# One transpose per pair for q and k in two units, and another order at the end of a hybrid attention block

## The chip, the cores and the metric

The kernel runs on one core of a Trainium2 chip. The metric is the device time of one execution in microseconds; lower is better. The time before is the median of three runs.

## The reference

The block has two attention branches over one RMS-normed input, `x` being 2048 positions of 1024 features in float32:

```
h    = rms_norm(x, norm_gain);  proj = h @ w_in
qa, ka, va, qb, kb, vb, ga, gb, mg = split(proj)
ya   = banded_attention(qa, ka, va, 128, ..., sink)       # A: 8 q heads, 2 kv heads
ya   = ya * silu(ga)
for g, (window, dilation) in ((128, 1), (512, 4), (2048, 16)):
    o, l = dilated_group(qb[g], kb[g], vb[g], window, dilation)   # B: 8 heads each
yb   = sum(softmax(lses) * outs) * silu(gb)
gates = sigmoid(mg + b_merge)
x    = x + (gates[0] * (ya @ w_branch_a) + gates[1] * (yb @ w_branch_b)) @ w_out
```

q and k of each head are RMS-normed over 64 features, and a bias by relative position is added to the scores.

## The kernel before

Every float32 operand is split into two float16 parts, and a product is made of three float16 products. The program is written out in full in one order: the code puts each step into a heap with a planned time (`at`), and `until` emits what is due. The planned times decide only the order of instructions on each engine; on the chip, engines wait for each other through semaphores.

**The attention stage.** It runs through 14 units (`UNITS`): two of kind A (4 q heads, 1 k and 1 v head, positions in 16 subsets of 128) and twelve of kind B (2 heads, one of the three dilations). A unit has 8 pairs, a pair has two subsets of 128 positions. `Pair.matmuls` projects them (line 697), and `Pair.plan` sets the steps behind it: `evac_qk`, the norm (`square` to `gain`), the split into `spl` (`hi`, `lo`), and `swap`, in which GpSimd (POOL) copies the k columns once more with the two parts exchanged (line 779). `spl` then holds two subsets of 6 blocks of 128 columns. `Pair.turn` (line 787) transposes it with one DMA per subset, issued on SyncE's queue (SP), into a tile `kq` of 6 blocks; there are 6 such buffers (`KQ_BUFS`), and for the first subset of a class of kind B with more than one subset a separate ring `kq0` of 3.

For each subset there are items of two heads. An item of kind A in the middle of the sequence reads its own `kq` and those of both neighbours (`Item.logits`, line 847), makes probabilities on VectorE and ScalarE, splits them (lines 875, 879), transposes them with a DMA on SP (line 885) into `pt16`, shown as `pt`, and multiplies them with v (`Item.values`, line 896). An item of kind A that has two neighbours transposes 1536 columns; a `kq` transpose has 768. SP issues all these transposes and all loads and stores of the stage, in the order of the program. Scores of an item come before the values of earlier items, so the transposes of several items are under way.

**The last stage.** Branch projections (`Branch`) and the output projection (`Out`) are made in 16 groups of 7 products each. A group makes four output blocks out of seven products (Strassen's scheme in Winograd's form). The products accumulate in three PSUM banks: products 0, 3, 5 and 6 in bank 0, products 1 and 4 in bank 2, product 2 in bank 1. `after` follows each product: in a `Branch`, 0, 1 and 3 are copied by ScalarE and 2, 4, 5 are added to a copy by VectorE (line 1854), 6 is used directly; in an `Out`, each product is added to the output tile by VectorE (`put`, line 2000), and four of the puts are followed by a store (line 2003). A product that accumulates into a bank waits until the value before it has been read.

`run` orders them: 0, 1, then the delayed product 5 of the group before (`late`), 2, 3, the delayed 6, 4; products 5 and 6 go into `pending`. `flush` emits what is pending, before the output group of step 6 and at the very end. So the products of the two groups in question come as (5', 6' being those of the neighbour): 0 1 5' 2 3 6' 4, later 5 6. `m_build` makes the operands `mf` of the output products out of the results of the branch groups.

Of the kernel before, what the change touches and what calls it, by code (L numbers as in the profile page):

```python
# [22 lines left out]
F16 = mybir.dt.float16  # L23
I32 = mybir.dt.int32
AF = mybir.ActivationFunctionType
OP = mybir.AluOpType
# [6 lines left out]
NT = S // 128  # L33
# [65 lines left out]
X_US = dict(look=0.25, land=4.3, next=1.45, late=.12, sq=1.14, st=.17, ln=.2, nw=.75, sc=1.24, tr=.8, hi=.5, lo=.62, gs=2.1, pw=1.3,  # L99
            gh=1.06, gl=1.26, mm=.217, th=.6, gt=.63, us=.83, uh=.75, ul=.82, ag=1.0, tl=1.3)  # L100
XT_BUFS = 14
KQ_BUFS = 6
VT_BUFS = 10
PT_BUFS = 4
N_BIAS_A = 384
# [3 lines left out]
def block_kernel(tc, x, w_units, w_gate, w_mrg, w_out, w_bra, w_brk, gain, qkg, sink, bias_a, bias_b, b_merge, out):  # L109
    nc = tc.nc  # L110
    V = nc.vector
    A = nc.scalar
    G = nc.gpsimd
    T = nc.tensor
# [12 lines left out]
    def ucol():  # L127

        ucount[0] += 1
        return ubuf[:, ucount[0] - 1:ucount[0]]  # L130
# [252 lines left out]
    def at(t, f, *args):  # L383
        seq[0] += 1
        heapq.heappush(heap, (t, seq[0], f, args))

    now = [0.0]

    def until(t):
        while heap and heap[0][0] <= t:  # L390
            now[0], _, f, args = heapq.heappop(heap)
            f(*args)
# [121 lines left out]
    class Order:  # L514
# [17 lines left out]
        def run(self):  # L532
            while self.steps:
                best = {}
                for n, s in self.steps.items():
                    t = self.start(n)
                    if t is not None:
                        best.setdefault(s[0], []).append((t, s[3], n))
                eng, c = min(best.items(), key=lambda e: min(e[1])[0])
                t0 = min(c)[0]  # L540
                t, _, n = min((x for x in c if x[0] <= t0 + (0 if eng == "T" else X_US["look"])), key=lambda x: x[1])
                eng, us, _, _, f, args, _ = self.steps.pop(n)
                self.end[n] = self.free[eng] = t + us
                at(t, f, *args)
# [15 lines left out]
    for t in range(NT):  # L560
        g = groups[t]
# [8 lines left out]
        for h in range(2):  # L570
            k = 2 * t + h
# [52 lines left out]
    wk = main.enter_context(tc.tile_pool(name="wk", bufs=2, reuse_waits="tile"))  # L624
# [55 lines left out]
    class Pair:  # L680
# [7 lines left out]
        def matmuls(self, i):  # L688
            un, (r, c) = self.un, self.subsets[i]
            self.ps[i] = ps = pj_p.tile([128, 512], F32, name="pj")  # L690
            out = []
            for a, b, aligned in ((0, 128, True), (128, 384, False)) if un.shift else ((0, 384, True),):
                h, lo = subset(0, un.g, r, c, aligned), subset(1, un.g, r, c, aligned)
                k = 0
                for ch in range(NCH):
                    for lhs, rhs in ((h, un.wh), (h, un.wl), (lo, un.wh)):
                        out.append(lambda lhs=lhs, rhs=rhs, ch=ch, a=a, b=b, k=k: T.matmul(  # L697
                            ps[:, a:b], lhsT=lhs[:, ch, :], rhs=rhs[:, ch, a:b], start=(k == 0), stop=(k == 23)))
                        k += 1
            return out  # L700
# [78 lines left out]
                G.tensor_copy(sp[:, i, nh:, :, :], sp[:, i, nq:nh, ::-1, :])  # L779

        def turn(self):
            for i, s in enumerate(self.subsets):
                if self.un.shift and s[1] == 0:
                    kq = wk.tile([128, 6, 128], F16, name="kq0", bufs=3)
                else:
                    kq = wk.tile([128, 6, 128], F16, name="kq", bufs=KQ_BUFS)
                nc.sync.dma_start_transpose(out=kq[:], in_=self.sp[:, i].rearrange("p a b c -> p (a b c)"))
                self.un.kq[s] = kq


    class Item:
# [415 lines left out]
    for u in range(NU + 1):  # L1207
        t = 8 * u
# [8 lines left out]
    for k in range(8):  # L1217
        u = 3 + k
        t = 8 * u
# [10 lines left out]
    t = 0  # L1230
    while t < NPAIR or heap or any(k >= t for k in fill):
        u, j = divmod(t, 8)
# [24 lines left out]
        for share, f, i, args in streams:  # L1257
            until(pos)
            if args is None:
                mm, after = f(i), ()  # L1260
            else:
                mm, after = f(*args)
            for k, m in enumerate(mm):
                until(pos + share * k / len(mm))
                m()
            pos += share
            for k, a in enumerate(after):
                at(pos + GATE[k], a)
# [35 lines left out]
    def bank():  # L1304
        return ps_p.tile([128, 512], F32, name="fps")

    (sb, ib), (so, io) = (scales[k] for k in "bo")
    ysg, yig, msc, bnd, i_o = (ucol() for _ in range(5))
# [420 lines left out]
    for k in range(2):  # L1729
        g = LAST - 2 + k  # L1730
# [36 lines left out]
    def y_build(s, k, b, b0=None):  # L1767
        load, sums, hi, lo = y_parts(s, k)
        at(b if b0 is None else b0, load)
        for n in range(4):  # L1770
            at(b + Y_S + .4 * n, sums, n)
        for n in range(7):
            at(b + Y_S + .9 + .7 * n, hi, n)
            at(b + Y_S + 1.7 + .7 * n, lo, n)
# [40 lines left out]
    class Seven:  # L1815
# [8 lines left out]
        def after(self, i):  # L1824
            b, r = self.b, self.r
            if i == 0:
                self.copy(0, b[0])
            elif i == 1:
                self.copy(2, b[2])
            elif i == 2:  # L1830
                self.sum(0, b[1])
            elif i == 3:
                self.copy(1, b[0])
            elif i == 4:
                self.sum(1, b[2])
            elif i == 5:
                self.sum(2, b[0])
            else:
                self.last(b[0])
# [16 lines left out]
    def emit(g, i):  # L1856
        until(pos[0])
        mm = g.mm(i)
        us = g.mm_us
        for k, m in enumerate(mm):  # L1860
            until(pos[0] + us * k / len(mm))
            m()
        pos[0] += us
        until(pos[0])
        now[0] = pos[0]
        g.after(i)

    pending = []

    def late():  # L1870
        if pending:
            emit(*pending.pop(0))

    def run(g):
        emit(g, 0)
        if g.n == 1:
            late()
            return
        emit(g, 1)
        late()  # L1880
        emit(g, 2)
        emit(g, 3)
        late()
        emit(g, 4)
        pending.extend(((g, 5), (g, 6)))

    def flush():
        while pending:
            pos[0] += .3
            late()  # L1890
# [5 lines left out]
    WO = rp.tile([128, 7, 2, 4, 512], F16, name="WO")  # L1896
# [78 lines left out]
    class Out(Seven):  # L1975
# [11 lines left out]
        def matmuls(self, i, ps, fresh):  # L1987
            m = mf[self.s, i]
            out = []
            for p in range(4):  # L1990
                for ml, wl in ((0, 0), (0, 1), (1, 0)):
                    k = len(out)
                    out.append(lambda p=p, ml=ml, wl=wl, k=k: T.matmul(  # L1993
                        ps[:], lhsT=m[:, ml, p, :], rhs=WO[:, i, wl, p, :],
                        start=(fresh and k == 0), stop=(k == 11), skip_group_check=True))
            return out

        def put(self, h, n, b, store=False):
            t = self.x[h, n]
            at(now[0] + .2, lambda: V.scalar_tensor_tensor(t[:], b[:], i_o[:], t[:], OP.mult, OP.add))  # L2000
            if store:
                t0 = 128 * self.s + 1024 * h
                at(now[0] + 1.0, lambda: nc.sync.dma_start(
                    out=out[t0:t0 + 128, 512 * n:512 * n + 512], in_=t[:]))

        def after(self, i):
            b = self.b
            for h, n, k, store in (((0, 0, 0, False),), ((1, 1, 2, False),), ((0, 0, 1, True),), ((0, 1, 0, False),),
                                   ((0, 1, 2, True),), ((1, 1, 0, True),), ((1, 0, 0, True),))[i]:
                self.put(h, n, b[k], store)  # L2010
# [3 lines left out]
    outs = [Out(s) for s in range(8)]  # L2014

    def AB(s):
        p = pos[0]
        at(p + (4.0 if s else 1.0), g_tiles, s, 1)
        if s == 0:
            at(p + 9, g_tiles, 1, 0)  # L2020
            for i in range(7):
                at(p + WO_AT[0] + WO_AT[1] * i, wo_load, i)
        run(Branch(s, 0))
        run(Branch(s, 1))

    AB(0)
    at(pos[0] + 9, outs[0].load, ((0, 0), (1, 1), (0, 1), (1, 0)))
    AB(1)
    for s in range(8):
        p = pos[0]  # L2030
        if s < 6:
            at(p + .1, g_tiles, s + 2, 0)
            y_build(s + 2, 0, p + 5.0, p + .05)
            y_build(s + 2, 1, p + 14.0)
        if s < 7:
            at(p + (24.0 if s < 6 else 2.0), outs[s + 1].load, ((0, 0), (1, 1)))
            at(p + (31.0 if s < 6 else 15.5), outs[s + 1].load, ((0, 1),))
            at(p + (31.1 if s < 6 else 28.0), outs[s + 1].load, ((1, 0),))
        if s == 6:
            flush()  # L2040
        run(outs[s])
        if s < 6:
            AB(s + 2)
    flush()
# [78 lines left out]
```

## Time and profile before

| | |
|---|---|
| median of 3 runs | 1914.71 us (1913.5 to 1917.62) |
| profiled execution | 1916.55 us |
| its span | 1914.3 us |
| granted TensorE clock, mean | 0.999 |
| matmuls | 19242 |
| DMA transposes | 224 `kq`, 256 `pt` |

The span runs from the first to the last profiled instruction; what lies around it (2.25 us) belongs to the execution's time. Lines of a timeline give start, length, engine, line, operation, tiles, count, and in brackets how long the engine stood idle before and what ended that. A row of stretches gives for each engine its busy time with its count of instructions, in the order PE, PEld, DVE, ACT, POOL, and then the granted clock, the share of the DMA engines and GB/s; a share over 1 is possible, since packets of one engine overlap.

### The profile page before, as it was taken

The page shows a single profiled execution, that of the slowest core. Times are in us where ns is not written, and L with a number is a line of the kernel's source. Part 1 is how long each engine was busy: PE and PEld are TensorE (multiplying, and loading weights), DVE is VectorE, ACT ScalarE, POOL GpSimd, SP SyncE. Part 2 cuts the span into 40 slices and gives each one's busy share as a digit, 9 for nine tenths or more (in the row PEclk, how much of TensorE's full clock was granted, in tenths as well). Part 3 has the DMA queues.
Part 4 walks back from the last instruction along what each step waited for, and adds up shares of the span by engine and source line. Part 5 has one row for each costly group of instructions (what it writes and reads, how often), then busy time and mean ns, then how long its engine had stood idle before and what let it go on. Part 6 is the DMA issues. An engine that isn't in the chain of part 4 may idle for free.

```text
span 1914.3 us, 51103 instructions
## 1 busy us (share of the span) xinstructions
PE 1873.9 (98%) x19242; PEld 1438.9 (75%) x19242; DVE 1500.7 (78%) x3835; ACT 1250.4 (65%) x3015; POOL 579.0 (30%) x1363
## 2 busy tenths in 40 slices
PE   6999999999999999999999999999999999999998
PEld 4567887889999899998999899544444446776774
DVE  7679878986887879878788888748679644987885
ACT  8577768887676777777776766565666865433431
POOL 1034343443454435534455444300000001322121
PEclk9999999999999999999999999999999999999999
DMA  6259998988889679888897777786666648854541
GB/s 256 83 98 197 164 185 134 192 161 178 149 161 181 134 158 200 151 170 169 143 179 144 147 154 132 165 309 172 211 198 188 190 156 273 290 164 122 148 148 65
DMA packets 639351, 326.21 MB, mean 170 GB/s; under 512 B 459264, under 2 KB 589952, under 8 KB 636672
## 3 DMA queue, kind: packets, MB, share of 16 engines
q1 hardware_dynamic: 638960, 322.70, 73.3%
q8 instruction: 150, 2.46, 0.6%
q14 instruction: 97, 0.79, 0.2%
q10 hardware_dynamic: 144, 0.26, 0.0%
HBM read 139.08 MB, written 73.66 MB: 111 GB/s over the span
## 4 chain that ended last, share of the span: by engine, by line
PE 90%; DMA 5%; DVE 2%; ACT 1%; issue 1%; POOL 0%; SPq 0%; DVEq 0%; POOLq 0%
PE pj L697 43%; PE fps L1602 17%; PE fps L1921 8%; PE fps L1993 8%; PE s L847 5%; PE pv L896 4%; DMA pt<-p 2%; PE pj L352 2%; PE pj L304 1%; PE fps L304 1%; DMA kq<-spl 1%; PE pt L960 1%; DMA bigl<-sd 1%; DVE pr L862 0%; PE s L482 0%
## 5 line engine op out<-in xcount | busy, mean ns | idle before, releaser
L697 PE MATMUL pj<-wl,XH 128*128 128x128 f16 (+2 forms) x2816 | 715.8, 268 | 0.0
L697 PE MATMUL pj<-wh,XL 128*128 128x128 f16 (+2 forms) x2816 | 712.2, 269 | 0.0
L697 PE MATMUL pj<-wh,XH 128*128 128x128 f16 (+2 forms) x2816 | 709.4, 268 | 0.0
L697 PEld LDWEIGHTS <-XH 128*128 128x128 f16 x5632 | 575.3, 112 | 54.5
L697 PEld LDWEIGHTS <-XL 128*128 128x128 f16 x2816 | 315.9, 112 | 24.0
L862 DVE CUSTOM_DVE_ANT_0 pr<-s,b,ubuf 128x256 f32<-128x256 f32 (+3 forms) x512 | 218.9, 465 | 44.1 <-PE s L847 41.7
L879 DVE SCALAR_TENSOR_TENSOR p<-pr,p 128x512 f16<-128x512 f32 (+2 forms) x256 | 195.7, 765 | 51.6 <-ACT p L875 50.4
L764 POOL TENSOR_TENSOR rw<-rw,g 128x128 f32<-128x128 f32 (+1 forms) x224 | 149.1, 686 | 202.5 <-DVE rw L757 183.2
L1931 POOL TENSOR_TENSOR g<-g,t 128x512 f32<-128x512 f32 x32 | 48.8, 1526 | 523.7 <-DVE t L1854 523.7
L1602 PEld LDWEIGHTS <-wh 128*128 128x128 f16 x1064 | 104.1, 99 | 123.5 <-issue 0.4
L715 ACT ACTIVATE rw<-pj 128x256 f32<-128x256 f32 (+1 forms) x224 | 87.5, 390 | 134.5 <-PE pj L697 134.0
L779 POOL COPY spl<-spl 128x256 f16<-128x256 f16 (+1 forms) x224 | 96.4, 460 | 246.5 <-DVE spl L774 246.5
L875 ACT ACTIVATE p<-pr 128x512 f16<-128x512 f32 (+2 forms) x256 | 157.7, 616 | 14.4 <-DMA pt<-p 10.1
L1921 PE MATMUL fps<-y,bigh 128*128 128x128 f16 x1792 | 153.5, 219 | 0.8 <-DVE r L1854 0.8
L847 PE MATMUL s<-kq 128*128 128x128 f16 (+1 forms) x1856 | 148.2, 218 | 4.8 <-DMA kq<-spl 3.9
L1921 PE MATMUL fps<-y,bigl 128*128 128x128 f16 x896 | 151.7, 219 | 0.0
L1993 PE MATMUL fps<-WO,mf 128*128 128x512 f16 x672 | 150.3, 379 | 0.8 <-DVE xr L2000 0.8
L847 PEld LDWEIGHTS <-kq 128*128 128x128 f16 x2016 | 131.0, 98 | 21.1 <-issue 5.7
L1921 PEld LDWEIGHTS <-bigh 128*128 128x128 f16 x1792 | 139.0, 98 | 8.2 <-issue 0.9
L896 PE MATMUL pv<-vt,pt 128*128 128x65 f16 (+1 forms) x2784 | 132.1, 193 | 8.7 <-DMA pt<-p 7.7
L896 PEld LDWEIGHTS <-pt 128*128 128x128 f16 x3024 | 119.6, 98 | 24.6 <-DMA pt<-p 12.5
L770 ACT ACTIVATE spl<-rw 128x512 f16<-128x512 f32 (+1 forms) x112 | 72.1, 643 | 79.7 <-POOL vt L726 71.4
(252 smaller groups left out, 3815.0 us busy)
## 6 DMA issues: line engine op xcount, KB each, us to landing
wraw<-in_w_units_dram SPq DMA_DIRECT2D x56, 384.0 KB, 4.8
g<-mgd SPq DMA_DIRECT2D x64, 256.0 KB, 5.4
wraw<-in_w_mrg_dram SPq DMA_DIRECT2D x45, 256.0 KB, 4.2
mgd<-t SPq DMA_DIRECT2D x43, 256.0 KB, 2.9
zd<-z SPq DMA_DIRECT2D x128, 66.0 KB, 2.0
zz<-zd SPq DMA_DIRECT2D x64, 132.0 KB, 3.5
xt<-in_x_dram SPq DMA_DIRECT2D x16, 512.0 KB, 7.8
ytd<-yo SPq DMA_DIRECT2D x32, 256.0 KB, 3.5
```

What stands on the lines that cost most here:

```text
L697: out.append(lambda lhs=lhs, rhs=rhs, ch=ch, a=a, b=b, k=k: T.matmul(ps[:, a:b], lhsT=lhs[:, ch, :], rhs=rhs[:, ch, a:b], start=(k == 0), ...
L715: A.activation(self.rw[:, n * i:n * i + n], self.ps[i][:, :n], AF.Copy)
L764: G.tensor_tensor(q[:, i, :un.nq, :], q[:, i, :un.nq, :], g, OP.mult)
L779: G.tensor_copy(sp[:, i, nh:, :, :], sp[:, i, nq:nh, ::-1, :])
L847: T.matmul(self.sv[j][:, o:o + k1 - k0], lhsT=q[:, h, :], rhs=kt[:, un.nq + kh + v * un.nk, k0:k1], start=(v == 0), stop=(v == 1))
L862: V.tensor_tensor_reduce(out=self.pv[:, j, self.p0:self.p0 + W], in0=self.sv[j], in1=un.bias[:, self.h0 + j, self.b0:self.b0 + W], scale=I ...
L875: A.activation(self.sp[:, :128 * n], self.pr, AF.Copy, scale=PSC)
L879: V.scalar_tensor_tensor(self.sp[:, 128 * n:], self.pr, PSC, self.sp[:, :128 * n], OP.mult, OP.subtract)
L896: T.matmul(self.po[:, j, :w], lhsT=p[:, n * j + s, :], rhs=un.v[key][:, vh, c0:c0 + w], start=(k == 0 and s == 0), stop=(k == 2 and s == n ...
L1602: T.matmul(b[k][:], lhsT=w[:, i, ch, :], rhs=xform(PROD[i][0], lo, ch, q), start=(i < 3 and n == 0), stop=(n == 11), skip_group_check=True)
L1921: out.append(lambda p=p, c=c, wl=wl, yl=yl, n=n: T.matmul(ps[:, 128 * p:128 * p + 128], lhsT=w[wl][:, i, c, p, :], rhs=y[:, yl, c, :], sta ...
L1993: out.append(lambda p=p, ml=ml, wl=wl, k=k: T.matmul(ps[:], lhsT=m[:, ml, p, :], rhs=WO[:, i, wl, p, :], start=(fresh and k == 0), stop=(k ...
```

## The change

It has two parts. In units of kind A a pair's two subsets are transposed by one DMA of 12 blocks. The tile `kq` holds a pair (12 blocks) in all units, with 4 buffers; units of kind B still issue two DMAs, each into its half. The ring `kq0` has one buffer, used only by the first subset of the undilated B unit.

In the last branch group (step 7, branch 1) and the last output group (step 7), `run` is called with `final`: the products come as 0 1 5' 3 2 6' 5 4, and only 6 stays pending. The very last product (step 7, product 6) is made in two halves of 256 columns: the right half alone into a new bank (`fb`), then the left half on top of bank 0. For that, the right half of bank 0 is added to the output tile after product 5, and each half has its own addition and its own store (`half`).

```diff
-KQ_BUFS = 6
+KQ_BUFS = 4
         def turn(self):
+            kq = wk.tile([128, 12, 128], F16, name="kq", bufs=KQ_BUFS)
+            outs = [kq[:, 6 * i:6 * i + 6] for i in range(2)]
+            if self.un.shift and self.un.n == NT and self.subsets[0][1] == 0:
+                outs[0] = wk.tile([128, 6, 128], F16, name="kq0", bufs=1)[:]
+            if self.un.kind == "A":
+                nc.sync.dma_start_transpose(out=kq[:], in_=self.sp[:].rearrange("p s a b c -> p (s a b c)"))
             for i, s in enumerate(self.subsets):
-                if self.un.shift and s[1] == 0:
-                    kq = wk.tile([128, 6, 128], F16, name="kq0", bufs=3)
-                else:
-                    kq = wk.tile([128, 6, 128], F16, name="kq", bufs=KQ_BUFS)
-                nc.sync.dma_start_transpose(out=kq[:], in_=self.sp[:, i].rearrange("p a b c -> p (a b c)"))
-                self.un.kq[s] = kq
+                if self.un.kind == "B":
+                    nc.sync.dma_start_transpose(out=outs[i], in_=self.sp[:, i].rearrange("p a b c -> p (a b c)"))
+                self.un.kq[s] = outs[i]
...
-    def run(g):
+    def run(g, final=False):
...
-        emit(g, 2)
-        emit(g, 3)
+        for i in (3, 2) if final else (2, 3):
+            emit(g, i)
         late()
-        emit(g, 4)
-        pending.extend(((g, 5), (g, 6)))
+        for i in (5, 4) if final else (4,):
+            emit(g, i)
+        pending.extend(((g, 6),) if final else ((g, 5), (g, 6)))
...
+            if (self.s, i) == (7, 6):
+                fb = bank()
+                for h in range(2):
+                    c, o = slice(256 - 256 * h, 512 - 256 * h), (fb[:, :256], ps[:, :256])[h]
+                    for p in range(4):
+                        for ml, wl in ((0, 0), (0, 1), (1, 0)):
+                            k = len(out)
+                            out.append(lambda p=p, ml=ml, wl=wl, c=c, o=o, h=h, k=k: T.matmul(
+                                o, lhsT=m[:, ml, p, :], rhs=WO[:, i, wl, p, c], start=(k == 0), stop=(k % 12 == 11),
+                                skip_group_check=True))
+                    if h == 0:
+                        out.append(lambda: self.half(1, fb[:, :256]))
+                return out
...
+        def half(self, j, b, store=True):
+            c, t0 = slice(256 * j, 256 * j + 256), 128 * self.s + 1024
+            t = self.x[1, 0]
+            V.scalar_tensor_tensor(t[:, c], b, i_o[:], t[:, c], OP.mult, OP.add)
+            if store:
+                nc.sync.dma_start(out=out[t0:t0 + 128, c], in_=t[:, c])
+
         def after(self, i):
             b = self.b
+            if (self.s, i) == (7, 6):
+                self.half(0, b[0][:, :256])
+                return
+            if (self.s, i) == (7, 5):
+                at(now[0] + .4, lambda: self.half(1, b[0][:, 256:], False))
...
-        run(Branch(s, 1))
+        run(Branch(s, 1), s == 7)
...
-        run(outs[s])
+        run(outs[s], s == 7)
```

## The prediction, made before the changed kernel ran

> **What bounds the kernel now.** I read the head of the page, then the list of waits for TensorE, then the two places that the change touches.
>
> ```profile
> span 1914.3 us, 51103 instructions
> PE 1873.9 (98%) x19242; PEld 1438.9 (75%) x19242; DVE 1500.7 (78%) x3835; ACT 1250.4 (65%) x3015; POOL 579.0 (30%) x1363
> PE 90%; DMA 5%; DVE 2%; ACT 1%; issue 1%; POOL 0%; SPq 0%; DVEq 0%; POOLq 0%
> ```
>
> TensorE is busy for all but 40.4 us of the span (1914.3 less 1873.9), and 90% of the chain is its own work. The change leaves every product in place, so it can only win idle time of TensorE, time lost to a low clock, and the tail behind the last product. What TensorE waits for (microseconds in all, times, longest):
>
> ```profile
> PE pv L896 <- DMA pt<-p: 7.7, 9, 2.0
> PE s L847 <- DMA kq<-spl: 3.9, 3, 1.6
> PE fps L1993 <- DVE xr L2000: 0.8, 1, 0.8
> PE fps L1921 <- DVE r L1854: 0.8, 1, 0.8
> ```
>
> The first row is the stake of the transposes: 7.7 us in nine waits for `pt`, the transposed probabilities. The last two rows are one wait each, at the ends of the two groups that are reordered. The three waits of the second row fall in units of kind B, whose transposes stay two per pair. Four of the nine, from TensorE's timeline (start, length, idle before in brackets):
>
> ```profile
> 182.42 0.71 PE L896 MATMUL pv<-vt,pt 128*128 128x65 f16 x18 [1.91 <-DMA pt<-p]
> 196.54 0.71 PE L896 MATMUL pv<-vt,pt 128*128 128x65 f16 x18 [0.37 <-DMA pt<-p]
> 201.89 1.15 PE L896 MATMUL pv<-vt,pt 128*128 128x65 f16 x18 [2.03 <-DMA pt<-p]
> 331.14 0.71 PE L896 MATMUL pv<-vt,pt 128*128 128x65 f16 x18 [0.60 <-DMA pt<-p]
> ```
>
> They lie in the two units of kind A. The stretches of these units, in busy time, clock, DMA share and GB/s, and 5 us for the next step:
>
> ```profile
> 100.00:160.00 60.00, 58.38 (x650) 41.20 (x647) 50.53 (x128) 48.71 (x113) 22.94 (x55) 1.00 0.71 123
> 160.00:205.00 45.00, 40.13 (x617) 36.76 (x615) 39.27 (x99) 34.43 (x78) 14.95 (x35) 0.97 1.11 207
> 300.00:330.00 30.00, 30.00 (x371) 22.34 (x370) 28.29 (x74) 26.98 (x63) 11.51 (x25) 1.00 0.83 138
> 330.00:390.00 60.00, 57.82 (x753) 47.45 (x751) 55.23 (x139) 50.88 (x119) 24.74 (x52) 1.00 1.07 190
> 200.00:205.00 5.00, 3.11 (x30) 2.58 (x31) 2.71 (x9) 2.92 (x6) 0.85 (x5) 0.69 1.16 172
> ```
>
> The losses are 4.9 us in the 45 us from 160 and 2.2 in the 60 from 330, and there the DMA engines are full (share over 1). So two things hold `pt` back: the queue on SP, which issues all transposes in order, and the DMA engines, which do the same bytes after the change. Only the first gets shorter.
>
> One more loss isn't idle time. Right behind the wait that ends at 201.89:
>
> ```profile
> 204.66 0.42 PE L697 MATMUL pj<-wl,XH 128*128 128x256 f16 x1
> 204.87 0.42 PE L697 MATMUL pj<-wh,XL 128*128 128x256 f16 x1
> ...
> 205.55 0.27 PE L697 MATMUL pj<-wh,XH 128*128 128x256 f16 x1
> 205.66 0.27 PE L697 MATMUL pj<-wl,XH 128*128 128x256 f16 x1
> ```
>
> The same product starts every 0.21 us first and every 0.11 afterwards: half clock, and a granted 0.69 from 200 to 205 means 3.1 of these 5 us, so from 201.9 on; it ends between 204.87 and 205.55. Some 3.4 us at half clock cost 1.7. The wait of 1.91 at 182.42 shows no such drop (the 45 us from 160 have 0.97, and 1.55 lost of 45 is that one drop alone). [...]
>
> **The transposes.** Rows of SP's queue and of the issues (ns least, median, most) and landings:
>
> ```profile
> 188.90 3.41 SPq L787 DMA_TRANSPOSE kq<-spl  x2
> 192.41 1.45 SPq L885 DMA_TRANSPOSE pt<-p  x1
> ...
> 323.62 2.57 SPq L787 DMA_TRANSPOSE kq<-spl  x2
> L787 SPq DMA_TRANSPOSE kq<-spl x13: 1226/1244/2057, 309.1 to 388.6; - x13
> DMA to landing us min/median/max: 2.8/2.9/5.6
> DMA to landing us min/median/max: 3.1/4.2/5.7
> ```
>
> A pair's two transposes hold SP for 2.57 us; one of twice the columns is what a `pt` of kind A already is (1536 columns, as `spl` has), and that takes 1.45. So each of the 16 pairs frees SP for 1.1 us. All of them would be 18 us, but it counts only where a `pt` that TensorE waits for stands behind. The landing rows are of 300 to 390 us, `kq` first, then `pt`: 2.9 us from issue to landing for one half, 4.2 for the long form. The second half lands 1.3+2.9 = 4.2 after the first issue today, so it lands when it did; the first half lands 1.3 later. The first half's cover is thinnest here (a pair's landing, its issue, and the first scores that read it):
>
> ```profile
> DMA to landing us min/median/max: 4.0/4.3/4.6
> 172.94 2.67 SPq L787 DMA_TRANSPOSE kq<-spl  x2
> 179.02 0.83 PE L847 MATMUL s<-kq 128*128 128x128 f16 x12
> ```
>
> The first half lands at 172.9+4.6 = 177.6; the second, issued half of 2.67 later, at 174.3+4.0 = 178.3. With one transpose the scores have 0.7 us left instead of 1.4. If that cover went, a pair would pay up to 1.3 us. The wait that is added, for the second `swap` too, costs nothing here: SP reaches the transposes late (behind a `pt`), not POOL.
>
> How much of the 7.7 us goes? In the first unit the `pt` at 192.41 stands directly behind a pair that held SP for 3.41 us, and waits at 196.54 and 201.89 follow: I take one pair's gain, 1.1 us, as moving the landing there, and none at 182.42, where the engines are full. In the second unit (2.2 us lost) the waits are 0.60 and less, below 1.1; with the engines at 1.07 I take half, 1.1. Then the wait at 201.89 falls to about 1 us, under the 1.91 that left the clock alone, and its 1.7 goes too. Sum 3.9 us; bounds 9.4 (all of 7.7 and 1.7) and, if the later first half or a longer block in the DMA queue makes waits of its own, minus 2 (one wait more that halves the clock, and a little).
>
> In units B the same DMAs are issued from the same places; the buffers (4 tiles of a pair, before 6 halves and 3 `kq0`) hold one pair more than a ring of 3 pairs did, and no wait of `kq` for a buffer stands among the waits of SP that matter. Nothing.
>
> **The last groups.** The rows of both ends, the last store, and a 256-column operation of the same kind on DVE:
>
> ```profile
> 1871.85 0.27 PE L1921 MATMUL fps<-y,bigh 128*128 128x128 f16 x2 [0.78 <-DVE r L1854]
> 1904.47 0.75 DVE L2000 SCALAR_TENSOR_TENSOR xr<-fps,ubuf,xr 128x512 f32<-128x512 f32 x1 [1.84 <-PE fps L1993]
> 1907.06 0.75 DVE L2000 SCALAR_TENSOR_TENSOR xr<-fps,ubuf,xr 128x512 f32<-128x512 f32 x1 [1.84 <-PE fps L1993]
> 1907.87 2.75 PE L1993 MATMUL fps<-WO,mf 128*128 128x512 f16 x12 [0.84 <-DVE xr L2000]
> 1910.65 0.75 DVE L2000 SCALAR_TENSOR_TENSOR xr<-fps,ubuf,xr 128x512 f32<-128x512 f32 x1 [2.84 <-PE fps L1993]
> L1763 DVE SCALAR_TENSOR_TENSOR y<-tq,ubuf,y 128x256 f16<-128x256 f32 x64 | 30.6, 483 | 5.2 <-ACT y L1759 5.2
> DMA to landing us min/median/max: 2.0/2.0/2.0
> 1897.90 0.38 SPq L1985 DMA_DIRECT2D xr<-in_x_dram  x1
> xr<-in_x_dram SPq DMA_DIRECT2D x1, 256.0 KB, 3.0
> ```
>
> Product 6 accumulates into the bank of product 5, so it waits until DVE has read that. With product 4 between (2.59 us in the last group, the distance of the DVE rows; about half of that in the branch group) both waits go: 0.78 and 0.84. Product 3 now comes one earlier, but the delayed product of the neighbour still lies between it and the copy that it needs. The last DVE operation shrinks from 0.75 to 0.48: 0.27. Its store takes 2.0 from issue to landing now; half the bytes may save up to 0.4, and I take 0. In halves product 6 is 24 steps at 0.11, 2.64 for 2.59: 0.05 more. The extra DVE addition after product 5 runs beside product 4. The new read of `x[1, 0]` behind product 5 comes at about 1903.7 (1907.06 less 0.78 and one product); its load is issued at 1897.90 today, lands at 1900.9 and moves ahead of a store in SP's queue, so 2.8 us cover it. Sum 1.84, say 1.8; bounds 1.6 and 2.3.
>
> Together 3.9 + 1.8 = 5.7 us. The profiled execution took 1916.55 (span 1914.3), 1.84 above the median of the runs; it would come out at 1910.85, and the median at 1909.0.
>
> **Rivals.** First, the transposes win nothing: where TensorE waits, the DMA engines are full, and the same bytes land at the same time. For it speaks the share of 1.11 and 1.07; against it that SP's block of 3.41 stands ahead of the late `pt`. Then only the last groups count: 1914.7 - 1.8 = 1912.9, or some 1911.5 with a part of the waits but the clock drop kept.
>
> Second, slower: the long transpose is a block of two halves in the DMA queue, issued before the `pt` behind it, and the first half's cover of 0.7 us is eaten. If in each of 16 pairs the next product waited 0.5 us more, that is 8.0, less 1.8: 1920.9. It turns into a loss of over 0.2% from 0.35 us per pair on (5.6 less 1.8). Against it: TensorE waits for `kq` at no place in units A today, and two halves land together with the long form.
>
> Third, SP alone holds `pt` back: then each pair's 1.1 us counts, and all of 7.7 and 1.7 goes: 1914.7 - 9.4 - 1.8 = 1903.5. For it speaks the block of 3.41, against it the full DMA engines.
>
> **How the numbers follow.** Forecast (waits shorter, clock drop gone) 0.44; transposes win little or nothing 0.37; slower by the block in the queue 0.12; all waits gone 0.07. A measurement of this kernel tells about 0.2% from no change, 3.8 us: faster means under 1910.9, which holds the first case and the last: 0.51. The second is within 0.2%: 0.37; slower 0.12. The range runs from 1904.5 (most of the waits gone) to 1916.0 (the last groups' gain, and waits of 3 us added).
>
> **What would show it.** In the profile after: one `kq` issue of about 1.45 us per pair in units A; the waits for `pt` in 180 to 205 and 330 to 390 us down from 7 to 4 or less; no half clock near 202; no waits of TensorE on DVE in the last 45 us; a last DVE operation of about 0.48. I am wrong if the waits for `pt` keep their sum, if TensorE waits for `kq` in units A, or if the clock drop only moves to another place.

## The result: 0.4% faster, and the profile after

| | before | after |
|---|---|---|
| median of the runs | 1915.3 us (6 runs) | 1908.49 us (6 runs, 1904.75 to 1911.12) |
| ratio, 95% interval | | 0.9961 (0.9947 to 0.9975) |
| profiled execution, its span | 1916.55, 1914.3 us | 1907.7, 1905.7 us |

A second set on another chip gave 1905.0 us (median of five runs) and 0.9955 (0.9942 to 0.9967); a sixth run, 1950.2 us at a granted clock of 0.949, is left out, and so is one run of the kernel before, 5057.78 us, from the ratios of e1, e2, e4 and e5. So the change wins 7.5 to 8.6 us (0.0039 and 0.0045 of some 1914; by the intervals 4.8 to 10.1 and 6.3 to 11.1). The prediction said 5.7 less, and 1909.0 us.

The head of the page after, and its chain by engine:

```profile
span 1905.7 us, 51101 instructions
PE 1871.5 (98%) x19254; PEld 1439.7 (76%) x19254; DVE 1500.6 (79%) x3837; ACT 1249.5 (66%) x3015; POOL 579.8 (30%) x1363
PE 90%; DMA 5%; DVE 2%; ACT 1%; issue 1%; POOL 0%; SPq 0%; DVEq 0%; POOLq 0%
```

TensorE's idle time fell from 40.4 to 34.2 us, its busy time by 2.4, of which a half-clock stretch that is gone makes 1.7 by the prediction's estimate. The waits of TensorE after (us in all, times, longest):

```profile
PE s L850 <- DMA kq<-spl: 4.9, 4, 2.3
...
PE pv L899 <- DMA pt<-p: 3.8, 5, 1.1
```

In this profile the waits for `pt` halved, 7.7 to 3.8 us, and those for `kq` rose by 1.0. The profile of the second set has the two the other way round:

```profile
PE pv L899 <- DMA pt<-p: 5.8, 6, 2.0
...
PE s L850 <- DMA kq<-spl: 2.5, 3, 1.9
```

All waits for `kq` still lie in units of kind B, whose transposes are issued as before. Both waits on VectorE in the last groups have left the list. The stretches of the units of kind A after (columns as in the prediction):

```profile
100.00:160.00 60.00, 58.89 (x659) 41.81 (x657) 50.53 (x127) 48.73 (x113) 22.95 (x55) 1.00 0.71 123
160.00:205.00 45.00, 43.18 (x711) 41.06 (x708) 43.36 (x110) 37.97 (x89) 16.53 (x37) 1.00 1.17 221
...
330.00:390.00 60.00, 59.31 (x773) 50.23 (x771) 56.58 (x148) 52.81 (x125) 24.78 (x52) 1.00 1.07 199
200.00:205.00 5.00, 5.00 (x98) 4.98 (x96) 4.96 (x12) 4.31 (x12) 0.87 (x2) 1.00 1.14 160
```

TensorE's idle time is 1.8 instead of 4.9 us in the 45 us from 160, and 0.7 instead of 2.2 in the 60 from 330. The clock stays at 1.00, and the DMA engines are as full as before (1.17 and 1.07): more bytes went through in the same stretch (221 for 207 GB/s) as the work ran earlier.

**Where the 8.6 us of the two profiles come from.** I compared the start of the same projection product in both traces. After is ahead by 0.7 us at 170, by 5.8 at 210, by 6.5 at 331, by 7.5 at 376 and by 8.5 at 543; then units of kind B give some back (7.2 at 786, 6.9 at 1194, 6.2 at the start of the last stage). The branch group adds 0.94 and the end 1.4. The comparison is with one profile of the kernel before: e2 and e3 below, which keep two transposes per pair, win 1.8 and 1.6 on that profile between 400 and 543 as well, so the 1.0 between 376 and 543 can't be put down to the change.

### The profile page after: what moved, and what is told of

Same layout as the page of the kernel before. It is cut to its first block, busy times and chain, and to the rows that moved or that the text cites. A ratio compares the mean times of both kernels' runs of the same rounds, so it can differ in the third digit from the quotient of the medians.

```text
span 1905.7 us, 51101 instructions
## 1 busy us (share of the span) xinstructions
PE 1871.5 (98%) x19254; PEld 1439.7 (76%) x19254; DVE 1500.6 (79%) x3837; ACT 1249.5 (66%) x3015; POOL 579.8 (30%) x1363
## 4 chain that ended last, share of the span: by engine, by line
PE 90%; DMA 5%; DVE 2%; ACT 1%; issue 1%; POOL 0%; SPq 0%; DVEq 0%; POOLq 0%
PE pj L697 43%; PE fps L1605 18%; PE fps L1925 8%; PE fps L2010 7%; PE s L850 5%; PE pv L899 4%; PE pj L352 2%; DMA pt<-p 2%; DMA kq<-spl 2%; PE pj L304 1%; PE fps L304 1%; PE pt L963 1%; DMA bigl<-sd 1%; PE s L482 0%; DMA graw<-in_w_gate_dram 0%
```

## The experiments

The experiments ran in three groups, each on one chip, beside runs of the kernel before on that chip: e1, e2, e4 and e5; e3, e6, e8 and e9; e10 and e11. Ratios are against those runs, and kernels of different groups are compared by their ratios. Diffs of e4, e5 and e8 are against e1, that of e11 against e8, those of e6 and e10 against the changed kernel, e2 and e3 against the kernel before; "..." marks lines left out.

### The two parts alone

The first, e1, has the new `turn` and `KQ_BUFS = 4`, and the old end:

```diff
-KQ_BUFS = 6
+KQ_BUFS = 4
...
+            if self.un.kind == "A":
+                nc.sync.dma_start_transpose(out=kq[:], in_=self.sp[:].rearrange("p s a b c -> p (s a b c)"))
```

> Only the new transposes and their buffers; the two last groups as before. If the gains of the two parts add up, as the profile after says (7.5 us won by 511 us into the span, 2.3 behind the attention stage, about 1 given back between), this is 4.5 to 6 us faster than before, ratio about 0.997, and TensorE's waits for pt are under 5 us with no half clock near 202 us. If the waits that go in units A come back later as waits for kq, it is 2 us or less.

Measured: 1909.01 us, 0.9973 (0.9962 to 0.9985), 5.2 us less. Against the expectation, its profile still has a half clock near 200 us, of which more below. The second, e2, has the other order and the halves, and the old `turn`:

```diff
-        run(Branch(s, 1))
+        run(Branch(s, 1), s == 7)
...
-        run(outs[s])
+        run(outs[s], s == 7)
```

> Only the order of the last two groups and the halves; transposes as before. Theory: 2.3 us faster (0.78 and 0.84 of waiting, 0.16 of a slower start behind the wait, 0.27 of the last operation, 0.24 of the last store), ratio 0.9988; the units of kind A keep their waits for pt of about 7.7 us and a half clock. Rival: the end is worth nothing outside one profile, ratio 1.000.

Measured: 1912.22 us, 0.9989 (0.998 to 0.9998), 2.1 us less. The parts add up: 7.3 us for 7.5 and 8.6. The waits for `pt`, first e1, then e2:

```profile
PE pv L899 <- DMA pt<-p: 4.6, 3, 2.1
```

```profile
PE pv L896 <- DMA pt<-p: 7.2, 7, 2.4
```

With the old transposes they keep 7 to 9 us (7.7 before, 7.2 here, 8.9 in e3 below), with the new they are 3.8 and 5.8 in the two profiles of the changed kernel and 4.6 in e1's. So the first rival (the transposes win nothing) is out: e1 alone is 2.9 to 7.3 us faster.

### The buffers without the long transpose

e3 has the tile of a pair with 4 buffers and the single `kq0`, but two DMAs in all units:

```diff
-                kq = wk.tile([128, 6, 128], F16, name="kq", bufs=KQ_BUFS)
+            kq = wk.tile([128, 12, 128], F16, name="kq", bufs=KQ_BUFS)
+            outs = [kq[:, 6 * i:6 * i + 6] for i in range(2)]
...
```

> Only the tiles: kq holds a pair in 4 buffers and kq0 has one, but units A issue two transposes per pair as before, and the two last groups are as before. Theory: the buffers do nothing, ratio 1.000 within 0.1%. Rival: the freer buffers are part of the gain, 2 us or more faster.

Measured: 1914.75 us, 1.0002 (0.9991 to 1.0013), with these waits:

```profile
PE pv L897 <- DMA pt<-p: 8.9, 8, 2.5
```

The buffers alone show no gain; the gain of e1 comes with the one DMA in the place of two.

### SP's queue or the DMA engines

The prediction had the queue on SP and the DMA engines both hold `pt` back, and only the queue get shorter. e4 was to fill SP's queue again, with three stores of 512 bytes behind each pair's transpose, one 4-byte element of each partition.

```diff
...
+                for _ in range(3):
+                    junk_n[0] += 1
+                    nc.sync.dma_start(out=junk[junk_n[0] - 1], in_=idf[:, 0:1])
```

> The new transposes alone (as in e1_transpose), and behind each pair's transpose in units A three stores of 512 bytes to a scratch tensor: about 1.1 to 1.5 us of SP's time per pair and next to no work for the DMA engines. Theory SP (the freed 1.1 us in SP's queue is what won): all of e1's gain in units A goes, so the time is that of before within 1 us, waits for pt back at 6 us or more. Theory engines (fewer or better packed packets won): still 4.5 to 6 us faster.

Measured: 1987.2 us, 1.0379 (1.0365 to 1.0392). This says nothing about SP, for with these stores there are stretches in which the DMA engines are busy for seven tenths and more and move only 6 to 35 GB/s. The waits for `pt`:

```profile
PE pv L904 <- DMA pt<-p: 55.8, 14, 6.8
```

The DMA engines from 130 to 150 us, busy tenths and GB/s in 40 slices of 0.5 us:

```profile
DMA  9009910499931079999999210999999999979999
GB/s 140 0 3 211 292 40 0 90 214 210 209 64 33 16 162 150 266 184 205 208 217 177 7 1 0 187 209 219 184 129 17 6 35 25 34 29 110 96 276 277
```

Such a stretch runs from 145 to 148 us (slices 31 to 36). The trace has 1108 packets of 256 bytes that take over 0.5 us in its units A (100 to 222 and 315 to 450 us), where e1's has 338 (100 to 195 and 285 to 375 us); the median packet of this size takes 0.02 us in both.

e8 is the same with stores of few rows: 16 rows of 512 bytes each.

```diff
...
+                for _ in range(3):
+                    junk_n[0] += 1
+                    nc.sync.dma_start(out=junk[junk_n[0] - 1], in_=idf[0:16, :])
```

> As e4_sp_time, but each of the three stores behind a pair's transpose in units A has 16 rows of 512 bytes instead of 128 of 4: 1.1 to 1.8 us of SP's time per pair and some 0.05 us of the DMA engines. Theory SP (the freed issue time won): the gain of the new transposes goes, the time is that of before within 1.5 us. Theory engines (one long transpose runs through the DMA engines better than two short ones): 4.5 to 6 us faster than before remain.

Measured: 1916.03 us, 1.0013 (1.0003 to 1.0023): all of e1's gain is gone, and 2.5 us (0.6 to 4.4) more, where the expectation allowed 1.5. Its waits for `pt`:

```profile
PE pv L904 <- DMA pt<-p: 10.2, 11, 2.0
```

SP's timeline, one pair's transpose and the stores behind it (start, length):

```profile
131.66 1.72 SPq L789 DMA_TRANSPOSE kq<-spl  x1
133.43 1.80 SPq L792 DMA_DIRECT2D junk<-idf  x3
```

The stores hold SP for 1.80 us per pair, somewhat more than the 1.1 that the change frees, and carry 24 KB. In the traces I split the time of the `pt` transposes of the units A, the last 24 of the 32 in each unit, into three parts: from the end of the split that makes `p` to the start of its issue, the issue, and from there to landing. Means in us, first unit, then second:

| | before the issue | issue | behind it |
|---|---|---|---|
| before | 1.51, 1.24 | 2.05, 1.76 | 2.83, 2.69 |
| e1 | 1.13, 0.65 | 1.99, 1.86 | 2.92, 2.55 |
| changed kernel, first profile | 0.74, 0.62 | 1.82, 1.88 | 3.00, 2.64 |
| changed kernel, second profile | 1.30, 0.75 | 1.89, 1.79 | 3.08, 2.62 |
| e8 | 2.01, 1.65 | 1.94, 1.80 | 2.88, 2.57 |
| e11 (below) | 0.97, 0.53 | 2.03, 1.81 | 2.82, 2.55 |
| e5 (below) | 1.57, 1.41 | 1.94, 1.92 | 2.93, 2.85 |

It is the time in the queue that moves: down by 0.2 to 0.8 with the long transpose, and in e8 up on e1 by 0.9 and 1.0 with the small stores. The issue and the transfer stay within 0.3 us. That is what a queue on SP that holds `pt` back looks like.

e11 makes e8's stores on ScalarE's queue: same bytes, no SP time.

```diff
-                    nc.sync.dma_start(out=junk[junk_n[0] - 1], in_=idf[0:16, :])
+                    nc.scalar.dma_start(out=junk[junk_n[0] - 1], in_=idf[0:16, :])
```

> As e8_sp_rows (the new transposes alone, and three stores of 16 rows of 512 bytes per pair in units A), but the three stores are issued on ScalarE's queue instead of SP's. Theory SP: the stores' bytes are nothing, SP keeps its freed time, 3.5 to 6 us faster than before (up to 1.5 us may go to ScalarE, which loses about 1 us per pair). Theory engines: the stores themselves cost the gain, the time of before within 1.5 us.

Measured: 1914.3 us, 1.0002 (0.9994 to 1.0011). By its time this missed. Its waits:

```profile
PE s L855 <- DMA kq<-spl: 4.2, 4, 2.2
PE pv L904 <- DMA pt<-p: 3.5, 4, 2.2
PE s L855 <- DVE nmA L870: 3.0, 6, 0.9
```

The issues on ScalarE's queue between 130 and 200 us (ns least, median, most):

```profile
L792 ACTq DMA_DIRECT2D junk<-idf x15: 308/453/812, 131.7 to 188.7; - x15
```

The waits for `pt` go from e8's 10.2 to 3.5 us, and the time before the issue from 2.01 and 1.65 to 0.97 and 0.53, as they should if SP's time was what e8 cost. But an issue holds ScalarE for a median 0.45 us, and the scores now wait 3.0 us for `nmA`, for which they waited 0.8 in e1 and in the changed kernel. So the queue times and the waits show SP's share; e11's time doesn't, since other prices took its place. Its profile is 5.8 us longer than e1's: the waits for `nmA` are 2.2 longer, those for `kq` 2.5 (0.8 of it in a unit A, at 179.36 us), those for `pt` 1.1 shorter, and there are two half-clock stretches in place of one, 1.7 more. Of these only the 2.2 points straight at ScalarE.

e5 loads the engines instead: one store of 384 KB per pair, the bytes of a pair's transpose.

```diff
...
+                junk_n[0] += 1
+                nc.sync.dma_start(out=junk[junk_n[0] - 1], in_=XH[:, 0:6, 0:256])
```

> The new transposes alone, and behind each pair's transpose in units A one store of 384 KB to a scratch tensor: some 0.4 us of SP's time and about 1.1 us of all DMA engines per pair. Theory SP: a third of e1's gain goes (0.4 of 1.1), 3 to 4 us faster than before remain. Theory engines: all of it goes and more, since the engines are full there: the time of before or up to 8 us slower.

Measured: 1917.55 us, 1.0019 (1.0009 to 1.0028), 8.8 us above e1, 0.55 per pair. The waits for `pt`:

```profile
PE pv L903 <- DMA pt<-p: 10.8, 10, 2.7
```

SP's timeline at the same place as in e8:

```profile
133.83 1.50 SPq L789 DMA_TRANSPOSE kq<-spl  x1
135.37 0.87 SPq L791 DMA_DIRECT2D junk<-XH  x1
```

By its time this is what theory engines expected, 3.6 us slower than before. The 1.1 us of all engines per pair in the expectation was the author's estimate, which no run shows; its 0.4 us of SP's time were too little. The store holds SP for 0.87 us, half of e8's 1.80, and costs about as much as e8's stores (8.8 and 7.7, with intervals that overlap). If SP's time costs what it did in e8 (7.7 for 16 times 1.80, so 0.27 per us), 3.7 of the 8.8 would be SP's and 5.1 the engines', by this estimate. The table above bears this out only in part: against e1 the time before the issue rises by 0.4 and 0.8 us, that behind it by 0.0 and 0.3. So by this estimate more bytes in these units cost time as well, but how much of the 8.8 is the engines' own isn't settled.

### One transpose per pair everywhere

e6 does in units of kind B what the change does in A, save for the pair whose first half goes to `kq0`:

```diff
-            if self.un.kind == "A":
+            one = self.un.kind == "A" or not (self.un.shift and self.un.n == NT and self.subsets[0][1] == 0)
+            if one:
...
```

> The changed kernel with one transpose per pair in units B as well (but for the first pair of an undilated unit). Theory: SP gets 1.1 us per pair back in 92 more pairs, but TensorE waits there only 3 to 5 us in all, for kq, and the first half lands 1.3 us later: within 2 us of the changed kernel. Rival 1, those waits go: 3 us faster than it. Rival 2, the later first half makes waits for kq in the undilated units: 5 us or more slower than it.

Measured: 1914.95 us, 1.0003 (0.9994 to 1.0012), against 0.9955 for the changed kernel on that chip: 9.2 us lost. Its waits:

```profile
PE s L851 <- DMA kq<-spl: 13.1, 10, 2.3
PE pv L900 <- DMA pt<-p: 2.5, 4, 0.9
```

The `kq` transposes of e6 from 700 to 900 us, their issues (ns least, median, most) and landing (us):

```profile
L788 SPq DMA_TRANSPOSE kq<-spl x21: 1274/1450/3302, 706.4 to 896.8; - x21
DMA to landing us min/median/max: 3.6/4.6/7.0
```

The same rows of the changed kernel:

```profile
L790 SPq DMA_TRANSPOSE kq<-spl x42: 1209/1238/2560, 701.4 to 893.5; - x42
DMA to landing us min/median/max: 2.7/3.7/6.8
```

SP issues half as many, and the waits for `pt` are the shortest of all kernels. But the first half lands 0.9 us later (4.6 for 3.7), and the waits of the scores for `kq` grow from 4.9 us (2.5 in the second profile of the changed kernel) to 13.1 in ten. Eight of the ten lie in the four undilated units, two in the first unit of dilation 4; there the scores are next before the transpose has landed. This is the second rival's mechanism, in units that the change spares.

### The change again, and a try for more

e9 is the changed kernel again, beside e3, e6 and e8.

> The changed kernel once more, beside the others on the same chip: 6 to 8 us faster than before; in its profile waits for pt of 3 to 5 us in all, and a half clock near 200 us in some executions, if the drop hangs on where the wait falls and not on the transposes alone.

It gave the 1905.0 us above, 8.6 us less, a little over what was expected. Its waits for `pt`, 5.8 us, are above the 3 to 5 expected; its profile has no half clock near 200 us, but two of its five runs have a granted clock of 0.999, as a run with one such stretch has. e10 takes loads off SP: those of the weights for two units and of `yo` go to ScalarE's queue.

```diff
-            nc.sync.dma_start(out=raw[:, 2 * i:2 * i + 2, :n], in_=src[:, 2 * i:2 * i + 2, :])
+            (nc.scalar if u in (1, 3) else nc.sync).dma_start(out=raw[:, 2 * i:2 * i + 2, :n], in_=src[:, 2 * i:2 * i + 2, :])
...
-            nc.sync.dma_start(out=self.o[:], in_=gtd[self.chunk][:, 512 * self.q:512 * self.q + 512])
+            nc.scalar.dma_start(out=self.o[:], in_=gtd[self.chunk][:, 512 * self.q:512 * self.q + 512])
```

> The whole change, and besides the plain loads of units A (the next unit's weights in four parts, and the gate blocks yo) are issued on ScalarE's queue: some 16 issues of about 0.5 us leave SP. Theory SP: the remaining waits for pt (4 to 6 us) shrink by half, 1 to 3 us faster than the changed kernel, ratio to before 0.9945. Theory engines: no difference from the changed kernel. Rival: ScalarE, busy for four fifths of these units, is held up by waits for a buffer or by the issues, and it is 2 us or more slower than the changed kernel.

Measured: 1908.04 us, 0.9967 (0.9957 to 0.9977), within the first interval of the changed kernel and at the edge of the second: the 1 to 3 us of theory SP didn't come. Its waits for `pt` are 3.0 us, those for `kq` 6.3 in its profile, one of them 2.2 us with a half clock behind it. No kernel here beats the change.

## Why the prediction was right, and where it was off

**The transposes: right mechanism, waits misplaced.** The sum had 3.9 us, e1 measured 5.2 (2.9 to 7.3), so the two agree within the noise; their parts don't. SP's timeline after, around one pair of the first unit:

```profile
183.94 1.41 SPq L888 DMA_TRANSPOSE pt<-p  x1
185.45 1.79 SPq L787 DMA_TRANSPOSE kq<-spl  x1
187.87 2.41 SPq L888 DMA_TRANSPOSE pt<-p  x1
```

The `kq` transposes after from 300 to 390 us, issues (ns) and landing (us; the landing row also holds two transposes of a unit of kind B):

```profile
L787 SPq DMA_TRANSPOSE kq<-spl x6: 1444/1594/1810, 303.4 to 370.1; - x6
DMA to landing us min/median/max: 2.8/4.0/5.8
```

The issue that was 3.41 for two is 1.79 for one. The median of 1.59 in the second unit is a little above the 1.45 taken, so a pair frees about 1.0 us of SP, as predicted. What was off is the next step, which waits move. The step said "none at 182.42, where the engines are full", put one pair's 1.1 us on the wait at 201.89, and took half of the second unit's. The same two products of the first unit after, from TensorE's timeline:

```profile
180.87 0.71 PE L899 MATMUL pv<-vt,pt 128*128 128x65 f16 x18 [1.07 <-DMA pt<-p]
197.72 0.71 PE L899 MATMUL pv<-vt,pt 128*128 128x65 f16 x18 [0.75 <-DMA pt<-p]
```

The second of them in the second profile, and the first in e1's (the other two are shown under the clock drop):

```profile
198.34 0.71 PE L899 MATMUL pv<-vt,pt 128*128 128x65 f16 x18 [1.61 <-DMA pt<-p]
180.95 0.71 PE L899 MATMUL pv<-vt,pt 128*128 128x65 f16 x18 [2.15 <-DMA pt<-p]
```

The wait at 182.42 was 1.91 and is 1.07, 2.05 and 2.15 in these three profiles (the changed kernel's two, then e1's); the one at 201.89 was 2.03 and is 0.75, 1.61 and 1.89. So "none at 182.42" held in two of three, and the 1.1 taken at 201.89 was 1.3, 0.4 and 0.1. What goes in all three are the short waits: the six at 154.21, 189.54, 196.54, 331.14, 344.40 and 374.56, each under one pair's 1.1, were 3.1 us together and are 0.2, 0.4 and 0.3. The same six are 1.4 in e2 and 3.5 in e3, which have two transposes per pair, 3.7 in e8, where stores fill SP again, and 0.6 in e11, where these are off SP. (The prediction read the waits of the second unit as "0.60 and less"; one more, at 385.02, was 0.68. A wait for `pt` of 0.6 to 1.1 near 224 us takes the place of one of 0.97 on ScalarE.)

From 100 to 230 us the lead over the profile before grew by 5.7, 3.7 and 1.9, which is 4.0, 2.0 and 1.9 without the 1.7 of the clock that the first two gained; from 230 to 376 by 1.8, 1.9 and 1.8. I had 1.1 for each unit: I counted one pair for a whole unit, and several waits got shorter. The engines' share over 1 doesn't cancel the queue's gain: in the table the time behind the issue stayed at 2.5 to 3.1 us, and the time before it fell.

**Given back.** In the profile of the changed kernel, 2.3 of the 8.5 us are lost again in units of kind B (8.5 to 6.2); in its second profile, from 9.0 to 8.0, it is 1.0. In its list of waits this shows as 4.9 for 3.9 us of `kq`; in its second profile the same waits are 2.5, so it isn't a steady price. So what units of kind B cost is not settled. I had "Nothing" for them, and e3 bears that out for the buffers.

**The clock drop: a wrong reason, and half of the term.** I let the 1.7 us go since the wait would be "under the 1.91 that left the clock alone". e1 has a wait there of 1.89, shorter than that, and its clock drops all the same. The wait in e1's timeline of TensorE:

```profile
199.38 0.71 PE L899 MATMUL pv<-vt,pt 128*128 128x65 f16 x18 [1.89 <-DMA pt<-p]
```

Two stretches of 3.41 us of e1:

```profile
196.79:200.20 3.41, 1.52 (x35) 1.36 (x33) 1.53 (x6) 1.79 (x6) 0.85 (x5) 1.00 1.33 166
200.20:203.61 3.41, 3.41 (x22) 2.54 (x20) 1.97 (x5) 2.98 (x8) 0.00 (x0) 0.50 0.98 189
```

And the second profile of the changed kernel has a longer wait, at the first of the two products, and keeps its clock:

```profile
180.46 0.71 PE L899 MATMUL pv<-vt,pt 128*128 128x65 f16 x18 [2.05 <-DMA pt<-p]
```

Two stretches of 3.41 us of that profile:

```profile
178.60:182.01 3.41, 1.55 (x33) 1.55 (x34) 3.41 (x7) 1.48 (x5) 1.58 (x3) 1.00 1.08 242
182.01:185.42 3.41, 3.41 (x59) 3.41 (x58) 3.19 (x9) 2.79 (x8) 1.34 (x5) 1.00 1.14 296
```

In these traces the drop went with the idle time within one stretch of a grid. In each trace the granted clock changes only at multiples of 3.413 us from the start of its record (before: that starts at 27.87 us, the clock falls 51 steps later at 201.94 and rises at 205.36). The first row of each pair above is such a stretch: TensorE is busy for 1.52 of the one (1.89 idle) and for 1.55 of the other (1.87 idle, the rest of the 2.05 fell into the stretch before), and only the first is followed by half clock (0.50). Before, the stretch from 198.53 has 2.02 idle and half clock behind it; in the first profile of the changed kernel the most in one stretch behind 27.97 us is 1.80 (from 1202.16), and the clock stays. Over the 12 profiles no stretch at full clock in the attention stage goes against this order. At half clock less idle was enough in e4, the one trace that shows it: a stretch at half clock with 1.04 us of idle or more was followed by another, and one with 0.44 or less by one at full clock. Behind the attention stage there is one exception, at the very end of e8 (from 1907.42, 1.98 us idle, no drop).

The wait of 1.91 at 182.42 before lay across a boundary, 0.96 on either side; the one at 201.89 did not. So the waits of 2.03 (before) and 1.89 (e1) cost 1.7 more, 3.41 us at 0.50, and those of 1.91 (before) and 2.05 (second profile) nothing, by where they fell. And the grid lay differently in these executions: from the start of the span a stretch begins 0.56 us behind a multiple of 3.413 before, 2.23 in e1 and 1.11 in the second profile. My threshold was a single case of luck.

Nor did the drop go for good: of the 70 runs of the kernel before beside the experiments 57 have a granted clock of 0.999 or 0.998, of the 11 of the changed kernel 5. One such stretch is 0.0009 of a run, so by these figures the mean falls from 0.94 stretches to 0.45, an estimated 0.8 us of the 1.7 in the sum (where in those runs the stretch lies is known from the profiles alone). That the sum came near is in part luck: its share for the queue, 2.2 us, was too small and that for the clock too large.

**The last groups.** 1.8 predicted, 2.1 measured in e2 (0.4 to 3.8), 0.94 + 1.4 = 2.3 in the profiles. VectorE's timeline at the end of the changed kernel:

```profile
1899.89 0.75 DVE L2017 SCALAR_TENSOR_TENSOR xr<-fps,ubuf,xr 128x512 f32<-128x512 f32 x1 [1.45 <-PE fps L2010]
1901.20 0.48 DVE L2026 SCALAR_TENSOR_TENSOR xr<-fps,ubuf,xr 128x256 f32<-128x256 f32 x1 [0.56 <-PE fps L2001]
1902.51 0.48 DVE L2026 SCALAR_TENSOR_TENSOR xr<-fps,ubuf,xr 128x256 f32<-128x256 f32 x1 [0.82 <-PE fps L2001]
```

TensorE's, the very last product in its two halves, with no wait ahead of it:

```profile
1899.69 2.78 PE L2001 MATMUL fps<-WO,mf 128*128 128x256 f16 x24
```

The landing of the last two stores:

```profile
DMA to landing us min/median/max: 1.8/1.8/1.8
```

The waits of 0.78 and 0.84 are gone and the last addition takes 0.48 (0.27 less), as in the sum. The store, taken at 0 out of "up to 0.4" (the author's estimate, which no row showed), lands in 1.8 instead of 2.0, 0.24 sooner before rounding. It was left out on the safe side. In the branch group the wait cost 0.94, and not its 0.78: products start every 0.06 us there, before the one ahead has ended, and the wait, which is counted from that end, also cost this overlap of 0.16. The sum lacked that.

**The rivals.** The first is refuted by e1. The second is not what happens in units A: there is no wait for `kq` there before or after. The landing row above mixes in two short transposes; the six pairs alone land 3.8 to 5.8 us after their issue, 4.8 in the median, where the prediction took 4.2. Before, the second half of a pair landed 4.7 and 4.6 us after the first issue (medians of the two units), and now the pair lands after 4.1 and 4.8, so only the first half comes later. Its cover was as thin as the prediction said: with the small stores added, e8 and e11 wait 0.31 and 0.79 us for `kq` near 179 us, the place it named. e6 shows this rival for units of kind B, at 9.2 us. The third, that all waits go, doesn't hold either: 3.8 and 5.8 us of waits for `pt` are left. What holds these back isn't shown; e5 speaks for the DMA engines, at a price that isn't settled.

## What to carry to other kernels

When a queue of DMA issues runs late, price an issue that falls out by all the waits behind it, and not by the one transfer next to it: here 1.1 us per pair took away nearly all of six waits that were shorter than that, in all three profiles, and left the two long ones at anything from 0.8 to 2.2. Before merging two transfers, ask whether someone waits for the first of them: the same merge won 5.2 us in the units A, where nobody did, and lost 9.2 in the units B, where the scores did. And don't judge a wait's effect on the clock by its length alone: here waits of 1.89 and 2.03 us cost 1.7 more and waits of 1.91 and 2.05 nothing, and what set them apart was the idle time within one stretch of 3.413 us (1.89 and 2.02, against at most 0.96 and 1.87).

## What the runs showed of the hardware

- In the attention stage TensorE fell from full to half clock for 3.41 us or more (1.7 us lost per stretch) after a stretch of a 3.413 us grid with 1.89 us (e1) and 2.02 us (before) of idle; 1.87 us (second profile of the changed kernel) left it at full clock. At half clock, 1.04 us of idle kept it there (e4).
- Issuing one transpose of 1536 columns held SP for a median 1.45 us, of 768 columns for 1.24 (the rows of e6 and the changed kernel above): twice the columns took 0.21 us more.
- A store of 128 rows of 4 bytes was no cheap filler. 48 of them cost 78 us against e1 (1.6 us each); 48 stores of 16 rows of 512 bytes, 16 times the bytes, cost 7.7. What made the short rows dearer was not tried.
